# A hybrid encoder step on one core: split input-projection weights kept in DRAM and read back

## Chip, cores and metric

One core of a Trainium2 chip. The metric is the device time of one execution in microseconds (us).

## What is computed

One layer of a streaming encoder on 2,048 prompt tokens and 8 x 16 sample tokens (2,176 rows of width 1,024, fp32). The part that matters here is the first step: one input projection whose columns go to three token mixers.

```python
proj = jnp.einsum('btd,de->bte', x, lp['w_in'])
qa, ka, va, qkv_b, beta_in, a_in, gate_b, u_c = jnp.split(proj, split_points(IN_SIZES), axis=-1)
...
out_a = band_attention_prompt(qa, ka, va, lp['a_rel_bias'])
ob, s_new = gated_delta_rule(qb, kb, vb, g, beta, s0)
y_c, h_re, h_im = s5_ssm(u, ...)
mix = jnp.concatenate([out_a, out_b, out_c], axis=-1) @ lp['w_out']
x = layer_norm(DN_ALPHA * x + mix, ...)
hid = jnp.square(jax.nn.relu(x @ lp['w_up'] + lp['b_up']))
x = layer_norm(DN_ALPHA * x + hid @ lp['w_down'], ...)
```

## The kernel before

`w_in` is cut into eleven column blocks of 256 (one, called G, of 264). Every fp32 operand of a large matmul is used in two parts, both of type fp32r: the high part is a cast on ACT (L60), the low part is what is left of the number, by a subtract on DVE (L61). One product of two such operands is three matmuls (`mm3`, L65 to L67: high x high, low x high, high x low).

`weights` (L206) brings one block: two loads of 512 KB into `wr` (two buffers), and from these four pairs of tiles `wh`, `wl`, each 128 x 512, that is two of the block's eight slices of the inner dimension. `wh` and `wl` have five buffers each, so that one pair of the next block can be made while the four of this block are in use; each later pair waits until the matmuls no longer read the pair whose buffers it takes. `feat` (L230) multiplies a block with the transposed x (output: features by tokens, one PSUM tile per 128 features and group of tokens, 24 matmuls each); `tok` (L252) gives tokens by features (24 matmuls per 128 tokens). The outputs go by ACT to a tile `st` and by DMA to DRAM.

The blocks are used over and over. `project1` goes over three ranges of tokens (768, 768, 640) and uses six blocks in each: 0 (input of the S5 mixer), G, 1, 2, 3, 8. In the third range it goes on with the five blocks 6, 7, 9, 4, 5 (`project2`, for the last 640 tokens), and `project2_all` goes over the other three ranges of 512 tokens with the same five. That makes 38 uses of 11 blocks: 11 first uses and 27 later ones. Each use loads and splits its block anew.

Beside these matmuls run the chunked delta rule (`deltanet`: names `cin`, `s`, `blk`, `Ti`, `TU`, `bqs`, `brs`, `bps`), from the end of the first range on, and the S5 mixer (`s5`: `Tm`, `U`, `yq`, `s5p`) during `project2_all`. `mix` (L127) interleaves them; a scheduler then fixes the order of the instructions on each engine. Every engine works through its instructions in that order. All DMAs are issued by SP, on one queue; a DMA that waits holds up those behind it. The DMAs take eight completion semaphores in turn, so that each waits also for the landing of the DMA eight places before it.

After this first part come attention, the output projection and the feed-forward part; the change touches none of their lines.

Of the kernel before, what the change touches and what calls it, by code (L numbers as in the profile page):

```python
# [9 lines left out]
F32 = mybir.dt.float32  # L10
F32R = mybir.dt.float32r
# [30 lines left out]
class K:  # L42
# [88 lines left out]
    def mix(self, upto):  # L131
        nc, A = self.nc, self.A
        bes, ses = ExitStack(), ExitStack()
        self.bp = self.pool("bp", 3, PSUM, es=bes, side="right")
        self.brp = self.pool("brp", 1, PSUM, es=bes, side="right")
        self.pp = self.pool("pp", 2, PSUM, es=ses)
        self.s5p = self.pool("s5p", 2, PSUM, es=ses)
        self.flip = 0
        self.parts_done = 0
        deltanet = self.deltanet()  # L140
        self.s5c = self.pool("s5c", 1, es=ses)
        with ExitStack() as es:
            dense = self.project1(es)
            next(dense)
            self.s5_setup()
            for _ in range(5):
                next(dense)
            self.parts_done = 1
            self.b_consts(bes)
            self.b_pools(bes)  # L150
            due = 0.0
            for i, _ in enumerate(dense):
                if i in (5, 11):
                    self.parts_done += 1
                due += PACE1 if i < 12 else PACE1B
                while due >= 1:
                    next(deltanet)
                    due -= 1
        with ExitStack() as es:
            self.merge((self.project2_all(es), 1.0), (deltanet, PACE_B), (self.s5(), PACE_C))  # L160
        nc.sync.dma_start(A["o_k"], self.kT[3])
        nc.sync.dma_start(A["o_v"], self.vS[3])
        ses.close()
        bes.close()
# [38 lines left out]
        self.w_p = self.pool(f"wp{n}", 3, es=es)  # L203
        self.st_p = self.pool(f"st{n}", 2, es=es)

    def weights(self, src, n=256):  # L206
        out = []
        for a in range(2):
            wr = self.w_p.tile([128, 4, n], F32, name="wr", tag="wr", bufs=2)
            self.nc.sync.dma_start(wr, src[:, a * 4:a * 4 + 4])  # L210
            for b in range(0, 4, 2):
                wh = self.w_p.tile([128, 2, n], F32R, name="wh", tag="wh", bufs=5)
                wl = self.w_p.tile([128, 2, n], F32R, name="wl", tag="wl", bufs=5)
                self.split(wh, wl, wr[:, b:b + 2])
                out += [(wh[:, k], wl[:, k]) for k in range(2)]
        return out

    def load_x(self, t0, groups):
# [10 lines left out]

    def feat(self, idx, x, groups, out, by_group=False, w=None):  # L230

        w = w or self.weights(self.A["w_inA"][idx])
        todo = [(m, z) for m in range(2) for z in range(len(groups))]
        if by_group:
            todo.sort(key=lambda mz: mz[1])
        for m, z in todo:
            n = groups[z][1]
            ms = slice(m * 128, (m + 1) * 128)
            ps = self.pp.tile([128, 512], F32, name="pps", tag="pp")
            for k in range(8):  # L240
                self.mm3(ps[:, :n], w[k][0][:, ms], w[k][1][:, ms], *x[k, z], k == 0, k == 7)
            out(m, z, ps[:, :n])
# [23 lines left out]
    def project1(self, es):  # L266

        nc, A = self.nc, self.A
# [2 lines left out]
        up = [upp.tile([128, 16, NC5], F32, name=f"up{m}") for m in range(2)]  # L271
        self.p_pools(es, 1)
        for j, (t0, T, groups) in enumerate(PARTS):
            w = self.weights(A["w_inA"][0])
            x = self.load_x(t0, groups)

            def keep_u(m, z, ps):
                n0, n = groups[z]
                c0 = (t0 + n0) // 16
                v = ps.rearrange("p (c t) -> p t c", t=16)  # L280
                nc.scalar.copy(up[m][:, 0:8, c0:c0 + n // 16], v[:, 7::-1])
                nc.vector.tensor_copy(up[m][:, 8:16, c0:c0 + n // 16], v[:, 15:7:-1])

            def keep_v(t, st):
                v, rows = self.at_a(self.vS, t0 // 128 + t)
                nc.sync.dma_start(v[rows, 0:256], st[:, :256])
                nc.sync.dma_start(self.baS[j][t * 128:t * 128 + 128], st[:, 256:264])

            self.feat(0, x, groups, keep_u, by_group=True, w=w)
            yield 2  # L290
            self.tok(A["w_inG"], 264, x, groups, keep_v)
            yield 2
            for i in range(3):
                self.feat(1 + i, x, groups, self.to_rows(self.bT[j], i * 256, 0, groups))
                yield 2
            self.feat(8, x, groups, self.to_rows(self.gT[j], 0, 0, groups), by_group=True)
            yield 2
            if j == 2:
                yield from self.project2(3, x, groups)
# [4 lines left out]
    def project2(self, j, x, groups):  # L304

        n = sum(n for _, n in groups)
# [4 lines left out]
        for a in range(2):  # L311
            self.feat(6 + a, x, groups, self.to_rows(self.kT[j], a * 256, 0, groups))
            yield n / 384
        self.tok(self.A["w_inA"][9], 256, x, groups, keep_v)
        yield n / 384
        for a in range(2):
            self.feat(4 + a, x, groups, self.to_rows(self.qT[j], a * 256, 0, groups, -0.125))
# [1617 lines left out]
```

## Time and profile before

| | |
|---|---|
| median of 3 runs | 2851.4 us (2848.71 to 2852.71) |
| profiled execution, its own time | 2849.91 us |
| its span in the profile | 2848.1 us |
| granted TensorE clock, mean | 0.991 |
| busy share of the span: PE, PEld, DVE, ACT, POOL | 96%, 84%, 68%, 46%, 36% |
| chain of work that ended last | PE 68%, DVE 16%, DMA 6%, issue 4%, ACT 3%, POOL 2%, SP queue 1% |
| moved by DMA | 355.55 MB, mean 125 GB/s |

The span is divided by what the code does: the projections with the delta rule and S5 end at about 920 us of the span, and everything after that is untouched. So the change is to be read in the first 920 us. PE is the matmul row, PEld the loading of its stationary operands. A matmul of 384 columns is shown as some 340 ns long although the next one starts 175 ns later; the busy share of PE therefore says little, the start times say more.

### The profile page before, as it was taken

To read this page: it belongs to the slowest core of one execution; us is meant where nothing else is said; L and a number is where in the kernel's file an instruction comes from. 1 tells how busy PE (TensorE), PEld (TensorE's weight loads), DVE (VectorE), ACT (ScalarE), POOL (GpSimd) and SP (SyncE) were. 2 spreads that over 40 slices of the span, in tenths; PEclk is the share of its full clock that TensorE was granted. 3 is DMA by queue.
4 is the path that set the end of the run, shared out by engine and by line. 5 is a ranking of instruction groups with operands and counts; after the bars stand their busy time and mean duration, and the time that the engine had idled before them with its cause. 6 is when DMAs were issued, how large, how long until landed. Compare 5 with 4: busy or idle time off the path is not lost.

```text
span 2848.1 us, 46357 instructions
## 1 busy us (share of the span) xinstructions
PE 2738.6 (96%) x16685; PEld 2405.1 (84%) x16685; DVE 1945.4 (68%) x4949; ACT 1305.6 (46%) x2714; POOL 1032.7 (36%) x914
## 2 busy tenths in 40 slices
PE   8999999989989899999999999999999999999998
PEld 8988888867677677788898998989989988999997
DVE  7587888788653788879855555576556557576766
ACT  3554554343355778612243443355334435444443
POOL 0010111232221232013354445345544453666664
PEclk9999999989999999999999999999999999999999
DMA  5644445555447652145631221153222214432321
GB/s 185 204 111 120 111 114 125 150 147 155 146 138 247 213 167 61 55 169 198 224 124 60 74 75 59 60 196 131 88 74 86 93 67 148 163 98 95 119 96 46
DMA packets 293436, 355.55 MB, mean 125 GB/s; under 512 B 85698, under 2 KB 218646, under 8 KB 292886
## 3 DMA queue, kind: packets, MB, share of 16 engines
q1 hardware_dynamic: 293206, 352.59, 39.4%
q8 instruction: 131, 2.15, 0.3%
q14 instruction: 99, 0.81, 0.1%
HBM read 280.25 MB, written 74.89 MB: 125 GB/s over the span
## 4 chain that ended last, share of the span: by engine, by line
PE 68%; DVE 16%; DMA 6%; issue 4%; ACT 3%; POOL 2%; SPq 1%; DVEq 0%; ACTq 0%; POOLq 0%
PE fdp L66 8%; PE fdp L65 8%; PE fdp L67 8%; PE pps L66 2%; PE pps L67 2%; PE pps L65 2%; PE fupz L67 2%; PE fupv L67 2%; PE fupv L65 2%; PE fupv L66 2%; PE fupz L65 2%; PE fupz L66 2%; PE fupx L65 2%; PE fupx L67 2%; PE fupx L66 2%
## 5 line engine op out<-in xcount | busy, mean ns | idle before, releaser
L1570 POOL TENSOR_TENSOR wu<-wur,wu 128x512 fp32r<-128x512 f32 x308 | 416.7, 1357 | 528.1 <-ACT wu L1569 527.4
L1696 DVE TENSOR_TENSOR fy<-fy,fdp 128x512 f32<-128x512 f32 x500 | 340.9, 685 | 255.8 <-PE fdp L67 255.5
L65 PE MATMUL fdp<-wdh,hh 128*128 128x512 f32 x1020 | 397.8, 390 | 1.2 <-DVE fy L1696 1.1
L66 PE MATMUL fdp<-wdl,hh 128*128 128x512 f32 x1020 | 397.3, 390 | 0.1
L67 PE MATMUL fdp<-wdh,hl 128*128 128x512 f32 x1020 | 397.1, 389 | 0.0
L1569 ACT CAST wu<-wur 128x512 fp32r<-128x512 f32 x308 | 189.6, 617 | 414.1 <-DMA wur<-in_w_upL 168.6
L65 PE MATMUL pps<-xh,wh 128*128 128x384 f32 (+2 forms) x800 | 279.6, 351 | 10.5 <-ACT xh L60 9.5
L66 PE MATMUL pps<-xl,wh 128*128 128x384 f32 (+2 forms) x800 | 279.3, 349 | 2.4 <-DVE xl L61 2.3
L67 PE MATMUL pps<-xh,wl 128*128 128x384 f32 (+2 forms) x800 | 277.1, 347 | 0.7 <-DVE wl L61 0.7
L65 PEld LDWEIGHTS fdp<-wdh,hh 128*128 128x128 f32 x1020 | 191.4, 188 | 41.0 <-DVE fy L1696 2.9
L67 PEld LDWEIGHTS fdp<-wdh,hl 128*128 128x128 f32 x1020 | 191.5, 188 | 40.0
L66 PEld LDWEIGHTS fdp<-wdl,hh 128*128 128x128 f32 x1020 | 191.5, 188 | 38.5 <-DVE wdl L61 0.7
L1643 DVE TENSOR_TENSOR hl<-fre,hh 128x384 fp32r<-128x384 f32 (+1 forms) x180 | 143.4, 797 | 85.1 <-ACT hh L1642 84.4
L60 ACT CAST wdh<-wdr 128x1024 fp32r<-128x1024 f32 x94 | 98.8, 1051 | 205.6 <-PE fdp L67 205.2
L65 PEld LDWEIGHTS pps<-xh,wh 128*128 128x128 f32 x800 | 151.9, 190 | 23.3 <-ACT xh L60 11.3
L61 DVE TENSOR_TENSOR wl<-wr,wh 128x512 fp32r<-128x512 f32 (+1 forms) x152 | 107.5, 716 | 86.3 <-ACT wh L60 84.2
L66 PEld LDWEIGHTS pps<-xl,wh 128*128 128x128 f32 x800 | 151.8, 190 | 14.3 <-DVE xl L61 5.5
L67 PEld LDWEIGHTS pps<-xh,wl 128*128 128x128 f32 x800 | 151.5, 189 | 12.4 <-DVE wl L61 2.5
L61 DVE TENSOR_TENSOR wdl<-wdr,wdh 128x1024 fp32r<-128x1024 f32 x94 | 133.1, 1421 | 6.6 <-ACT wdh L60 6.6
L60 ACT CAST wh<-wr 128x512 fp32r<-128x512 f32 (+1 forms) x152 | 92.3, 618 | 79.9 <-DMA wr<-in_w_inA 41.4
L1638 ACT ACTIVATE fre<-fre,ld_b_up 128x384 f32<-128x384 f32 (+1 forms) x144 | 85.9, 597 | 63.3 <-DVE fre L1647 40.3
L1229 ACT ACTIVATE P<-P,st 128x640 f32<-128x640 f32 (+4 forms) x128 | 97.2, 760 | 30.2 <-DVE st L1226 29.6
(569 smaller groups left out, 7241.7 us busy)
## 6 DMA issues: line engine op xcount, KB each, us to landing
wdr<-in_w_dnL SPq DMA_DIRECT2D x96, 512.0 KB
wur<-in_w_upL SPq DMA_DIRECT2D x88, 512.0 KB
wr<-in_w_inA SPq DMA_DIRECT2D x70, 512.0 KB
TU<-tD SPq DMA_DIRECT2D x34, 256.0 KB
y<-in_x SPq DMA_DIRECT2D x17, 512.0 KB
x<-y SPq DMA_DIRECT2D x17, 512.0 KB
fxr<-x SPq DMA_DIRECT2D x17, 512.0 KB
fy<-x SPq DMA_DIRECT2D x17, 512.0 KB
```

Source lines behind the costliest of these rows:

```text
L60: nc.scalar.copy(hi, src)
L61: nc.vector.tensor_tensor(lo, src, hi.bitcast(F32), OP.subtract)
L65: mm(out, lh, rh, start=first, stop=False, **kw)
L66: mm(out, lh, rl, start=False, stop=False, **kw)
L67: mm(out, ll, rh, start=False, stop=last, **kw)
L1229: self.nc.scalar.activation(x, x, AF.Exp, scale=-1.0, bias=st[:, q:q + 1], accum_out=st[:, 2 + q:3 + q])
L1569: self.nc.scalar.copy(hi, src)
L1570: P.tensor_tensor(lo, src, hi.bitcast(F32), OP.subtract)
L1638: nc.scalar.activation(r, src, AF.Relu, bias=self.bu[:, c * 2 + i:c * 2 + i + 1])
L1643: V.tensor_tensor(hl, r, hh.bitcast(F32), OP.subtract)
L1696: V.tensor_tensor(y, y, ps[x], OP.add)
```

## The change

`weights` now takes the number of the block (None for G) and keeps, per block, four DRAM tiles of 2 x 128 x 512. At the first use of a block it loads and splits as before and then writes the high and the low part of each pair to DRAM: eight DMAs of 256 KB. At every later use it neither loads nor splits; it reads the eight parts back straight into `wh` and `wl`.

```diff
+        self.wD = {}
...
-    def weights(self, src, n=256):
+    def weights(self, i, n=256):
+        nc = self.nc
+        first = i not in self.wD
+        if first:
+            self.wD[i] = [self.dram.tile([2, 128, 2 * n], F32, name=f"wD{i}_{a}") for a in range(4)]
         out = []
-        for a in range(2):
-            wr = self.w_p.tile([128, 4, n], F32, name="wr", tag="wr", bufs=2)
-            self.nc.sync.dma_start(wr, src[:, a * 4:a * 4 + 4])
-            for b in range(0, 4, 2):
-                wh = self.w_p.tile([128, 2, n], F32R, name="wh", tag="wh", bufs=5)
-                wl = self.w_p.tile([128, 2, n], F32R, name="wl", tag="wl", bufs=5)
-                self.split(wh, wl, wr[:, b:b + 2])
-                out += [(wh[:, k], wl[:, k]) for k in range(2)]
+        for a in range(4):
+            w = wh, wl = [self.w_p.tile([128, 2, n], F32R, name="w" + q, tag="w" + q, bufs=5) for q in "hl"]
+            if first:
+                if a % 2 == 0:
+                    wr = self.w_p.tile([128, 4, n], F32, name="wr", tag="wr", bufs=2)
+                    src = self.A["w_inG"] if i is None else self.A["w_inA"][i]
+                    nc.sync.dma_start(wr, src[:, a * 2:a * 2 + 4])
+                b = a % 2 * 2
+                self.split(wh, wl, wr[:, b:b + 2])
+            for q in range(2):
+                t = w[q].rearrange("p k n -> p (k n)").bitcast(F32)
+                if first:
+                    nc.sync.dma_start(self.wD[i][a][q], t)
+                else:
+                    nc.sync.dma_start(t, self.wD[i][a][q])
+            out += [(wh[:, k], wl[:, k]) for k in range(2)]
         return out
```

The calls pass the number in place of the source. Of the DMAs of `weights`, 76 loads of `wr` before become 22 loads, 88 writes and 216 reads of 256 KB.

How the instructions move shows at two places of SP's queue. The first is the start of the program (`xr` is a raw tile of x, of which the first product needs eight). Before:

```order
L71 DMA ld_c_ident<-in_c_ident 128x128
L210 DMA wr<-in_w_inA 128x1024 x2
L225 DMA xr<-in_xT 128x384 x6
L71 DMA ld_s_are<-in_s_are 128x16
L71 DMA ld_s_aim<-in_s_aim 128x16
```

After:

```order
L71 DMA ld_c_ident<-in_c_ident 128x128
L221 DMA wr<-in_w_inA 128x1024 x2
L240 DMA xr<-in_xT 128x384 x4
L227 DMA wD_0_126<-wh 128x512
L227 DMA wD_0_126<-wl 128x512
L227 DMA wD_1_127<-wh 128x512
L227 DMA wD_1_127<-wl 128x512
L227 DMA wD_2_128<-wh 128x512
L227 DMA wD_2_128<-wl 128x512
L227 DMA wD_3_129<-wh 128x512
L227 DMA wD_3_129<-wl 128x512
L240 DMA xr<-in_xT 128x384 x12
```

Eight writes, each of which waits for its half of a split, now stand between the fourth and the fifth tile of x.

The second place is the change from block G to block 1 in the second range (`st_2154` and `st_2218` are G's fifth tile of tokens; `blk`, `cin`, `DT` belong to the delta rule; in brackets the semaphores waited for). Before:

```order
L210 DMA wr_2900<-in_w_inA 128x1024 [waits DMAHW0_49,DVE_49]
L505 DMA cin_2744<-bT0_60 128x131 [waits DMAHW1_49,DMAHW2_49,DVE_49,Activation_49]
L605 DMA aD_81<-at_1965 64x4x64 [waits DVE_49]
L605 DMA aD_81<-at_1965 64x4x64 [waits DMAHW3_49]
L286 DMA vS2_76<-st_2183 128x256 [waits DMAHW4_49,Activation_49]
```

After:

```order
L229 DMA wh_2519<-wD1_1_832 128x512 [waits DMAHW7_49,PE_49]
L621 DMA blk_1738<-aD_81 32x16x16 [waits DMAHW4_49,DMAHW3_49,DMAHW0_49]
L301 DMA vS2_76<-st_2247 128x256 [waits DMAHW1_49,Activation_49]
L302 DMA baS1_79<-st_2247 128x8 [waits DMAHW2_49]
L229 DMA wl_2520<-wD1_1_832 128x512
L229 DMA wh_2523<-wD1_2_833 128x512 [waits PE_49]
L229 DMA wl_2524<-wD1_2_833 128x512 [waits DMAHW5_49]
L229 DMA wh_2527<-wD1_3_834 128x512 [waits DMAHW6_49,PE_49]
L229 DMA wl_2528<-wD1_3_834 128x512 [waits DMAHW7_49]
L520 DMA cin_2804<-bT0_60 128x131 [waits DMAHW0_49,DVE_49]
```

Where a load into `wr` waited for DVE to be done with the raw tile, reads into `wh` and `wl` now wait for PE to be done with the pair before, with the delta rule's loads behind them.

## Rows read from the trace of the kernel before

**Rows 1.** Stretches, us from the start: busy time and instructions by engine, clock, DMA
```profile
core 0: us, PE busy (x) PEld busy (x) DVE busy (x) ACT busy (x) POOL busy (x), PEclk, DMA share, GB/s
0.00:30.00 30.00, 21.12 (x114) 20.44 (x115) 22.32 (x100) 16.62 (x35) 0.20 (x4) 1.00 0.79 254
30.00:98.00 68.00, 67.84 (x425) 67.12 (x424) 38.79 (x150) 18.94 (x37) 1.55 (x6) 1.00 0.60 175
98.00:430.00 332.00, 319.58 (x2385) 286.65 (x2384) 268.15 (x1069) 177.50 (x457) 46.15 (x53) 1.00 0.45 124
430.00:580.00 150.00, 145.50 (x1090) 126.87 (x1089) 115.57 (x442) 59.45 (x153) 32.72 (x69) 1.00 0.49 133
580.00:860.00 280.00, 247.59 (x1513) 199.06 (x1512) 204.97 (x607) 119.31 (x260) 72.23 (x95) 0.95 0.52 151
860.00:920.00 60.00, 58.91 (x301) 48.65 (x299) 17.53 (x30) 30.17 (x56) 6.39 (x6) 1.00 0.79 256
```

**Rows 2.** Costliest groups of the page: the splits of the weights
```profile
L61 DVE TENSOR_TENSOR wl<-wr,wh 128x512 fp32r<-128x512 f32 (+1 forms) x152 | 107.5, 716 | 86.3 <-ACT wh L60 84.2
L60 ACT CAST wh<-wr 128x512 fp32r<-128x512 f32 (+1 forms) x152 | 92.3, 618 | 79.9 <-DMA wr<-in_w_inA 41.4
```

**Rows 3.** Waits, 0 to 920 us: total us, times, longest us
```profile
ACT wh L60 <- PE pps L66: 28.6, 36, 4.1
...
SPq L210 <- DVE wl L61: 26.2, 20, 6.2
```

**Rows 4.** Waits of PE, 98 to 430 us
```profile
PE brs L786 <- DVE Ti L627: 2.7, 3, 1.5
...
PE pps L67 <- DVE wl L61: 0.3, 1, 0.3
```

**Rows 5.** Chain of waits by line: of 98 to 430 us, then of 580 to 920 us
```profile
by line: issue 11.3%; PE bqs L649 8.7%; PE pps L67 7.1%; PE pps L66 7.1%; PE pps L65 6.9%; DVE s L512 5.7%; DVE tp L625 2.9%; DMA wr<-in_w_inA 2.7%; PE brs L692 2.7%; PE brs L690 2.6%; DVE Ti L627 2.6%; DVE wl L61 2.5%; PE brs L694 2.3%; PE
...
by line: issue 7.0%; DMA yq<-yS 5.5%; PE pps L66 5.1%; PE pps L67 4.9%; PE pps L65 4.8%; DMA rv<-in_relrev 4.2%; DMA Tm<-kS 3.8%; DMA xr<-in_xT 2.8%; PE s5p L1019 2.4%; DVE s L512 2.3%; DVE wl L61 2.3%; PE bqs L649 2.2%; DVE xl L61 2.2%; SP
```

**Rows 6.** Pieces of that chain: start us, us, what
```profile
226.66 4.45 DMA wr<-in_w_inA
...
231.13 0.63 ACT wh L60
...
231.79 0.69 DVE wl L61
...
238.63 3.60 DMA TU<-tD
...
288.61 5.26 DMA xr<-in_xT
```

**Rows 7.** Timeline of the start: SP's issues and ACT's first casts
```profile
2.12 3.09 SPq L225 DMA_DIRECT2D xr<-in_xT  x6
...
7.79 2.85 ACT L60 CAST xh<-xr 128x384 fp32r<-128x384 f32 x6
```

**Rows 8.** Timeline of PE: matmuls of 384, of 264 and of 512 columns
```profile
12.20 0.34 PE L66 MATMUL pps<-xl,wh 128*128 128x384 f32 x1
...
14.14 0.34 PE L65 MATMUL pps<-xh,wh 128*128 128x384 f32 x1
14.31 0.34 PE L66 MATMUL pps<-xl,wh 128*128 128x384 f32 x1
...
27.92 0.28 PE L65 MATMUL pps<-wh,xh 128*128 128x264 f32 x1
28.04 0.29 PE L66 MATMUL pps<-wl,xh 128*128 128x264 f32 x1
...
902.22 0.39 PE L66 MATMUL pps<-xl,wh 128*128 128x512 f32 x1
902.45 0.39 PE L67 MATMUL pps<-xh,wl 128*128 128x512 f32 x1
```

**Rows 9.** DMA issues: KB each
```profile
TU<-tD SPq DMA_DIRECT2D x34, 256.0 KB
```

More of the change, by code (lines that the diff above doesn't have):

```diff
@@ L230, in feat @@
     def feat(self, idx, x, groups, out, by_group=False, w=None):
-        w = w or self.weights(self.A["w_inA"][idx])
+        w = w or self.weights(idx)
         todo = [(m, z) for m in range(2) for z in range(len(groups))]
@@ L273, in project1 @@
         for j, (t0, T, groups) in enumerate(PARTS):
-            w = self.weights(A["w_inA"][0])
+            w = self.weights(0)
             x = self.load_x(t0, groups)
@@ L290, in project1 @@
             yield 2
-            self.tok(A["w_inG"], 264, x, groups, keep_v)
+            self.tok(None, 264, x, groups, keep_v)
             yield 2
@@ L313, in project2 @@
             yield n / 384
-        self.tok(self.A["w_inA"][9], 256, x, groups, keep_v)
+        self.tok(9, 256, x, groups, keep_v)
         yield n / 384
```

## The prediction

> **What bounds the kernel now.** I read first the stretches of the span, cut where the code goes from one kind of use to the other [rows 1]: 0 to 98 us holds the first uses of six blocks, 98 to 430 us twelve later uses, 430 to 580 us five first uses, 580 to 920 us fifteen later ones. The reader is to see that PE is the engine in use nearly all the time. In 98 to 430 us it is idle for 332.0 - 319.6 = 12.4 us and its weight loads for 45.4 us; in 580 to 860 us for 32.4 and 80.9 us; before 98 us (the first 30 us apart) and from 860 us on it is hardly idle at all. DVE is second, at 268.2 of 332.0 us. DMA has room in the middle (shares 0.45 to 0.52) and little at both ends (0.79).
>
> Then the groups of instructions [rows 2]: each split is a cast of 618 ns on ACT and a subtract of 716 ns on DVE. Then who waits for whom. The casts wait 36 times for PE to free a pair, 28.6 us in all, and SP's loads 20 times for DVE to be done with a raw tile, 26.2 us [rows 3]; but PE waits directly for a low part for only 0.3 us in 98 to 430 us, and its longest item there is 2.7 us [rows 4]. The splits matter through the chain instead: in those two stretches it runs through `wl` for 2.5% of 332 and 2.3% of 340 us [rows 5], because DVE takes its work in order and the delta rule's small operations stand behind `wl`. One such place is shown [rows 6]: a load of 4.45 us, a cast of 0.63, a subtract of 0.69, and the solve goes on only then.
>
> **What the change removes (G).** 27 later uses x 4 splits = 108 casts and 108 subtracts: 108 x 0.618 = 66.7 us of ACT and 108 x 0.716 = 77.3 us of DVE [rows 2]. On the chain this is at most 2.5% x 332 + 2.3% x 340 = 16.1 us of `wl`, some 4 us of `wh` (7 pieces of 0.6 us, of which one is shown [rows 6]) and 2.7% x 332 = 9.0 us of `wr` [rows 5]: 29 us. The gain lies between 0, where PE is busy anyway, and 29 us. Since PE is idle for only 12.4 us in the first of the two stretches and waits there for other things [rows 1, 4], I take 8 us: nearer to the direct waits than to the chain.
>
> **The start (S).** The eight writes of block 0 now stand ahead of the fifth tile of x. Before, six tiles were issued from 2.12 us on, and their casts ran without a gap from 7.79 us [rows 7], so that the fifth was cast at about 7.8 + 4 x 0.475 = 9.7 us. The writes are 8 x 0.262 = 2.1 MB; 254 GB/s at a share of 0.79 [rows 1] is 322 GB/s at full share, so they take 6.5 us, and the fifth tile comes at about 16.2 us. The first four tiles give PE 24 matmuls, which end at about 12.2 + 12 x 0.175 = 14.3 us (twelve had been started by 12.20 us, 0.17 us apart from there on [rows 8]). The rest is a stall of 2 us, 3 with the tile's own split. Bounds: 0, if the writes start late enough to let x pass in the DMA engines, and 8, if all eight tiles of the second group come late too. PE is full until 98 us, so this is not made up. I take 3 us.
>
> **Later first uses (F).** Blocks G, 1, 2, 3, 8 write 10.5 MB in 30 to 98 us, 154 GB/s on top of 175 GB/s. That stretch moved 175 GB/s at a share of 0.60, so full share is between 292 GB/s and the 322 of the start [rows 1]: 329 GB/s needs 1.02 to 1.13 times the stretch, 1 to 8 us more. Loads made ahead for the second range can give way; lower bound 0, I take 3. The writes of 430 to 580 us (10.5 MB, 70 on top of 133 GB/s at 0.49) find room: 0, covered by PE, which is full there; without that cover they would be late by their own 7 parts in 100 of the stretch at most. A write waits for its split, and behind it on SP stand stores and the next block's load, which is still a whole use (17 us of PE) ahead.
>
> **The read-backs (B), the largest term.** A pair may be overwritten only when the last output tile of the use before has gone past it. Matmuls of 384 columns start 0.175 us apart, of 264 0.12, of 512 0.23 [rows 8]; a pair serves six of them, so in the last tile of 24 the pairs come free 1.05, 0.73 or 1.37 us apart. The first pair of the next block has spare buffers; the second, third and fourth don't. Before, ACT and DVE refilled such a pair in 0.62 + 0.72 = 1.3 us. Now a DMA does. The trace has no such read; the nearest row is `TU`, of the same 256 KB [rows 9], which landed after 3.60 us [rows 6]. The second half follows 0.262 MB / 322 GB/s = 0.8 us later, and so does each further one.
>
> For 384 columns the second pair is full at 1.05 + 3.6 + 0.8 = 5.45 us from the start of the last tile, the fourth at 8.65; PE wants them at 4.2 + 1.05 = 5.25 and 4.2 + 3.15 = 7.35. That is 1.3 us late. After G (last tile 2.9 us) it is 2.3 us; from one block to the next at 512 columns the fourth is full at 8.97 and wanted at 5.5 + 4.1 = 9.6, so in time; after a block of `tok` 1.3 us late. The uses: 10 x 1.3 + 2 x 2.3 + 3 x 1.3 + 12 x 0 = 21.5 us, if nothing stands between. But about half of the 2,385 matmuls in 98 to 430 us are the delta rule's [rows 1], and they stand between the projection's: I take two thirds, 14 us. Lower bound 0. Upper bound: a load that shared the queue landed after 5.26 us instead of 3.6 [rows 6]; 1.66 us more at each change gives 10 x 3.0 + 2 x 4.0 + 3 x 3.0 + 12 x 1.1 = 60 us.
>
> The Trainium skill, "DMA: Bandwidth & Descriptors", section "Anatomy of one DMA", gives a fit of about 2.0 us plus the bytes at 436 GB/s (measured on another issuing path), 2.6 us for 256 KB; the row says 3.60, and the sum goes by the row. By the page each change would be 1.0 us earlier and B an estimated 4 us.
>
> The added wait and what is behind it: the read waits at SP's head for PE, and behind it stand the other half, the delta rule's `blk` and `cin` and stores of `st`. Loads waited there before too, for DVE [rows 3]. 250 more DMAs also wait each for the landing of the eighth before. I put nothing on this beyond the bounds of B.
>
> **The end of the part (T).** From 860 us on PE is full and the projections run alone; 5.5 uses read 1.05 MB more each, 96 on top of 256 GB/s, which is 352 against 256 / 0.79 = 324 GB/s [rows 1]: 60 x 352 / 324 = 65 us, 5 more. Loads for attention can give way: 0 to 6, I take 3. The Trainium skill, same page, section "Where 436 GB/s comes from", puts the ceiling of the DMA engines at 435 GB/s; by it there would be room, and T would be 0. The row bears out only 324, by its busy share.
>
> **Sum.** S 3 + F 3 + B 14 + T 3 - G 8 = 15 us. On the profiled execution's 2849.9 us this is 2864.9; the median of the runs is 1.5 us above that execution, so I predict **2866 us**. A difference under 0.2% (5.7 us) is about what a measurement of this kernel can't tell from no change.
>
> **Rivals.**
> - *The vector engines are freed and the reads hidden (faster).* The chain's 29 us come off, since no `wl` stands ahead of the solve any longer, and the delta rule's matmuls cover B but for 3 us: 2851.4 - 29 + 3 + 6 (S and T) = 2831 us. For it: DVE at 268 of 332 us, and the piece at 226 us [rows 1, 6]. Against it: the 12.4 us that PE has to give there, and PE's own waits [rows 4]. It decides if pairs land before PE comes to them, that is within 3.1 us of being freed at 384 columns.
> - *Gain and cost cancel (same).* B 3 and G 8 with S and F and T as above in part: 2851.4 - 8 + 3 + 6 = 2852 us. For it: matmuls of another kind at every change of block.
> - *The queue becomes the bound (much slower).* Reads that wait for PE hold SP, each landing comes late by the upper bound: S 8, F 8, B 60, T 3, no gain but 8: 2851.4 + 71 = 2922 us. For it: the 5.26 us row; against it: shares of 0.45 and 0.52 in the stretches with later uses [rows 1].
>
> That the change doesn't do what it says is excluded by the order of the instructions (22 loads, 88 writes, 216 reads).
>
> **How the numbers follow.** Chances: forecast 0.46, freed engines 0.25, cancel 0.17, queue 0.12. Faster 0.25, same 0.17, slower 0.46 + 0.12 = 0.58. The forecast's own range is 2856 to 2890. The range given, 2834 to 2904, takes in the forecast and "cancel" and part of the other two: of "faster" its smaller gains, of "queue" its lower end; some 0.2 stay outside.
>
> **What would show it.** ACT's casts and DVE's subtracts of weights fall from 152 to 44 each, DVE in 98 to 430 us by about 35 us. PE's first wait after the start is for a cast of x, near 14 to 17 us. In the stretches with later uses PE's waits on projections name a DMA out of the kept tiles, 0.5 us each on average. The part ends near 935 us; the rest of the span takes as long as before. The prediction is wrong if PE's idle time in 98 to 430 us falls below 12 us (then G is larger and B hidden), or if SP's waits for PE come to more than 100 us (then the queue bounds).

## The result, and the profile after

| | before | after |
|---|---|---|
| median of the runs | 2850.7 us (2848.7 to 2852.7) | 2922.8 us (2921.4 to 2923.9) |
| span of the profiled execution | 2848.1 us | 2922.0 us |
| granted TensorE clock, mean | 0.991 | 0.979 |

The change makes the kernel 1.0258 times as long (95% interval 1.0245 to 1.0271), 72 us. The forecast was 15 us: the sign was right, the size far off, and the time lies outside the range.

The page of the kernel after: engines, DMA queue, chain by engine. Then the splits of the weights, by tile (count, shortest/median/longest ns, first and last start).

```profile
PE 2766.0 (95%) x16685; PEld 2423.2 (83%) x16685; DVE 1891.3 (65%) x4841; ACT 1250.4 (43%) x2606; POOL 1030.7 (35%) x914
...
q1 hardware_dynamic: 329206, 404.12, 43.7%
...
PE 69%; DVE 13%; DMA 8%; ACT 3%; issue 3%; POOL 2%; SPq 1%; DVEq 0%; ACTq 0%; POOLq 0%
```

```profile
L61 DVE TENSOR_TENSOR wl<-wr,wh x44: 673/690/701, 6.3 to 621.0; 128x512 fp32r<-128x512 f32 x40, 128x528 fp32r<-128x528 f32 x4
```

The 108 subtracts are gone, and DMA's share of the chain has gone from 6% to 8%. Where the time went is read by stage. The start of the last evacuation of a use (ACT's copy of its last PSUM tile, a row of the timeline) is the same event in both traces. It comes at 117.3 us before and 121.3 after for the last first use of range one, 460.7 and 511.8 for the end of the third range's first six blocks, 597.0 and 640.7 for that of its five further ones, 626.5 and 695.6 for the first use of `project2_all`, 856.4 and 914.4 for the tenth, 919.9 and 983.7 for the last. So the shift is **4, 51, 44, 69, 58, 64 us**, and the first result of attention is 74 us later. From there on both kernels take 1917 us. All of the loss stands in the first part, and it comes in steps. In the middle the shifts are not lost time alone, since other work changes places too: by 511.8 us PE has done 1,404 matmuls that aren't the projections', by 460.7 us before 1,310. By the tenth use of `project2_all` it has done 2,581 in both.

The stretches of [rows 1], in the kernel after, cut at the same events, and one more up to attention (PE, PEld, DVE, ACT, POOL busy; clock; DMA share; GB/s):

```profile
0.00:32.00 32.00, 20.88 (x98) 19.42 (x98) 18.78 (x79) 15.83 (x34) 0.20 (x4) 1.00 0.83 272
32.00:104.00 72.00, 69.58 (x429) 68.94 (x430) 42.37 (x167) 18.12 (x35) 1.55 (x6) 0.98 0.83 274
104.00:466.00 362.00, 333.18 (x2391) 297.64 (x2389) 247.88 (x1041) 154.87 (x412) 44.93 (x53) 0.95 0.55 156
466.00:626.00 160.00, 151.71 (x1137) 131.66 (x1137) 119.63 (x454) 61.45 (x158) 34.78 (x71) 0.98 0.60 174
626.00:918.00 292.00, 248.33 (x1467) 199.29 (x1467) 174.09 (x537) 94.45 (x212) 65.70 (x93) 0.92 0.64 194
918.00:984.00 66.00, 59.97 (x297) 47.97 (x295) 7.04 (x14) 16.78 (x31) 1.04 (x2) 1.00 0.81 271
984.00:1005.00 21.00, 13.49 (x62) 7.98 (x62) 6.28 (x36) 11.98 (x34) 7.90 (x10) 0.58 0.73 220
```

Two things are to be seen. PE's idle time in the stretch of the twelve later uses is 362.0 - 333.2 = 28.8 us; it was 12.4 [rows 1]. And the clock column falls below 1.00 in five of the seven rows; before it did so in one of six. A share of 0.95 over 362 us is 36 us at half the clock (only 0.5 and 1 occur); the rows add up to about 110 us, those of before to about 36 up to the same event. PE was busy in 78 us of these (27 before).

The 74 us up to attention's first result have two parts. PE is idle for 107.9 us, and was for 62.9: 45 us. And it is busy for 896.8 us, and was for 867.5, with the same matmuls: 29 us. At half the clock a matmul of 384 columns starts 0.32 us after the last one in place of 0.175 (rows below), so the 51 us more of work at 1.2 GHz in place of 2.4 cost an estimated 23 us of these 29.

PE's waits, 0 to 1005 us (total, times, longest), and SP's:

```profile
PE bqs L664 <- DMA TU<-tD: 15.8, 3, 10.9
PE pps L65 <- ACT xh L60: 10.6, 3, 8.5
PE pps L65 <- DMA wh<-wD: 8.3, 7, 3.9
PE s5p L984 <- DVE WB L979: 7.1, 1, 7.1
...
PE pps L66 <- DMA wl<-wDNone: 5.2, 2, 3.4
...
PE pps L67 <- DMA wl<-wD: 2.5, 6, 0.9
```

```profile
SPq L229 <- PE pps L67: 19.7, 29, 4.1
...
SPq L227 <- ACT wh L60: 16.0, 10, 3.3
```

With two small groups (1.3 and 0.7 us) the waits that name a read-back come to 18.0 us. SP's waits for PE at the reads are 19.7 us, and 7 more on another semaphore, far under the 100 us that the prediction had named as the sign of a bound by the queue.

How a late refill looks, on PE's timeline (in brackets the idle time before the row and what ended it):

```profile
186.47 0.45 PE L67 MATMUL pps<-xh,wl 128*128 128x384 f32 x1 [0.93 <-DMA wl<-wD]
...
187.10 0.50 PE L67 MATMUL pps<-xh,wl 128*128 128x384 f32 x2
188.55 0.69 PE L65 MATMUL pps<-xh,wh 128*128 128x384 f32 x1 [0.95 <-DMA wh<-wD]
189.03 0.52 PE L66 MATMUL pps<-xl,wh 128*128 128x384 f32 x1
189.35 0.52 PE L65 MATMUL pps<-xh,wh 128*128 128x384 f32 x1
...
191.90 0.34 PE L66 MATMUL pps<-xl,wh 128*128 128x384 f32 x1
192.07 0.34 PE L65 MATMUL pps<-xh,wh 128*128 128x384 f32 x1
```

After the wait the matmuls start 0.32 us apart, where [rows 8] have 0.175 for this size, and from 191.90 on 0.17 again: the granted clock is 0.5 from 188.5 to 191.9 us. A wait of 0.95 us cost some 1.5 us more in slow matmuls.

The refills themselves, pieces of the chain of waits from 117 to 480 us (start, us, what):

```profile
122.82 4.26 DMA wl<-wD
...
143.50 5.87 DMA wh<-wDNone
...
183.87 4.63 DMA wh<-wD
...
253.35 2.90 DMA wl<-wD
```

Seven such pieces stand in that stretch, 2.9 to 5.9 us long, 4.1 in the mean; the forecast took 3.6 us from `TU` [rows 6]. The Trainium skill, "DMA: Bandwidth & Descriptors", section "Anatomy of one DMA", has a fit, measured on another issuing path, by which 256 KB take an estimated 2.6 us; the measured pieces decide against it here.

The first step behind the first range, 10 us at the first use of the second (24.1 us long, 14.1 before): PE waits for the first pair of block 0, and SP issues its read only at the end of the first range, where the load of block 0 had gone out 21 us ahead. PE and SP after, then SP before:

```profile
125.08 0.66 PE L65 MATMUL pps<-xh,wh 128*128 128x384 f32 x1 [3.85 <-DMA wh<-wD]
```

```profile
121.11 0.82 SPq L229 DMA_DIRECT2D wh<-wD  x1
```

```profile
96.47 0.38 SPq L210 DMA_DIRECT2D wr<-in_w_inA  x1
```

What stands ahead of it in the queue, constants and the zeroing of `tD`, went out from 71 to 94 us before and goes out from 83 to 121 us now; up to 105 us SP waits some 20 us for halves to be written. The granted clock is 0.5 from 123.6 to 130.4 us.

The largest single step, 25 us at the first use of `project2_all`: SP's issues, then PE.

```profile
638.34 3.06 SPq L264 DMA_DIRECT2D qT<-st  x2
641.44 1.81 SPq L317 DMA_DIRECT2D uS<-up  x3
656.18 1.90 SPq L650 DMA_DIRECT2D tD<-Ti  x4
658.19 2.07 SPq L651 DMA_DIRECT2D TU<-tD  x4
660.32 0.97 SPq L240 DMA_DIRECT2D xr<-in_xT  x2
661.33 0.43 SPq L229 DMA_DIRECT2D wh<-wD  x1
```

```profile
640.28 0.28 PE L67 MATMUL pps<-xh,wl 128*128 128x256 f32 x1
647.62 1.11 PE L984 MATMUL s5p<-ld_c_ident,WB 128*128 128x128 f32 x4 [7.06 <-DVE WB L979]
648.66 1.89 PE L990 MATMUL s5p<-ZC,st 128*16 128x256 f32 x4
661.42 1.97 PE L664 MATMUL bqs<-at,TU 128*128 128x64 f32 x8 [10.87 <-DMA TU<-tD]
```

The projections end at 640.6 us. SP then stands from 643.3 to 656.2 before the delta rule's `tD`, which waits for DVE to finish `Ti`, and the tiles of x for the next range stand behind it. PE has nothing else to do: two holes of 7.1 and 10.9 us, and the clock at 0.5 until 673 us. Before, x was issued from 593.8 us, ahead of `tD` and `TU`. No read-back is late here; the scheduler's order on SP is another. Of the 25 us some come back: 71 more matmuls of other work stand ahead of the end of this use than before, and by the tenth use the shift is 58.

### The profile page after: what moved, and what is told of

It is laid out like the page before. It is cut to its first block, busy times and chain, and to the rows that moved or that the text cites. A ratio compares the mean times of both kernels' runs of the same rounds, so it can differ in the third digit from the quotient of the medians.

```text
span 2922.0 us, 46500 instructions
## 1 busy us (share of the span) xinstructions
PE 2766.0 (95%) x16685; PEld 2423.2 (83%) x16685; DVE 1891.3 (65%) x4841; ACT 1250.4 (43%) x2606; POOL 1030.7 (35%) x914
## 3 DMA queue, kind: packets, MB, share of 16 engines
q1 hardware_dynamic: 329206, 404.12, 43.7%
## 4 chain that ended last, share of the span: by engine, by line
PE 69%; DVE 13%; DMA 8%; ACT 3%; issue 3%; POOL 2%; SPq 1%; DVEq 0%; ACTq 0%; POOLq 0%
PE fdp L66 8%; PE fdp L65 8%; PE fdp L67 8%; PE pps L67 3%; PE pps L66 3%; PE pps L65 3%; PE bqs L664 2%; PE fupv L67 2%; PE fupv L65 2%; PE fupv L66 2%; PE fupz L65 2%; PE fupz L67 2%; PE fupz L66 2%; PE fupx L65 2%; PE fupx L67 2%
## 5 line engine op out<-in xcount | busy, mean ns | idle before, releaser
L67 PEld LDWEIGHTS pps<-xh,wl 128*128 128x128 f32 x800 | 153.0, 191 | 16.7 <-DMA wl<-wD 6.2
L66 PEld LDWEIGHTS pps<-xl,wh 128*128 128x128 f32 x800 | 153.2, 192 | 12.4 <-DVE xl L61 3.1
L199 ACT ACTIVATE st<-pps 128x384 f32<-128x384 f32 (+3 forms) x122 | 57.1, 468 | 206.0 <-PE pps L67 164.1
L1241 DVE CUSTOM_DVE_ANT_0 P<-aps,nb 128x128 f32<-128x128 f32 (+3 forms) x128 | 60.3, 483 | 78.8 <-PE aps L1240 78.5
```

What stands on the lines that cost most here:

```text
L66: mm(out, lh, rl, start=False, stop=False, **kw)
L67: mm(out, ll, rh, start=False, stop=last, **kw)
L1241: self.nc.vector.tensor_tensor_reduce(x[:, x0:x0 + n], ps[:, d0:d0 + n], nb[:, x0:x0 + n], 1.0, low, OP.add, OP.min, st[:, q:q + 1])
```

## Experiments

The theories, as the expectations name them. **R**: refills are late, because a pair can be read back only after PE has freed it. **Q** and **B**: places in the queue, and bytes. **O**: the scheduler's other order, at `project2_all` above all, where x stands behind `tD` and `TU`. **H**: a write that waits for its split holds the queue, and the loads behind it can no longer run ahead. Shifts are against before, at the events named above; "over before" is the median less that of before, measured beside it on the same chip. The edits are given in short.

### Which half of the change costs

**Writes alone.** Every later use loads and splits as before.

```diff
-            if first:
+            if True:                     # load wr and split, always
...
-                else:
-                    nc.sync.dma_start(t, self.wD[i][a][q])
```

> First uses write their 88 halves to DRAM, but the later uses load and split as before; nothing is read back. Theory R (refills come late: a pair can be read back only after PE has freed it, lands 3 to 5 us later, PE stalls and then runs at half its clock): only the start and the first uses pay, as in the profile after, where the evacuations were 4 to 8 us later up to 121 us; total 4 to 10 us over before, 2855 to 2861 us, PE's half-clock time in the first 930 us near that of before (46 us). Theory Q (250 more DMAs and 86 MB more on one queue hold up all the others): 88 of the 250 cost their share of the 72 us, some 25 us: 2876 us. Theory O (the scheduler puts other work behind other work; above all x of project2_all stands behind the delta rule's TU on SP): in this program x stands ahead of TU again, so the step of 25 us at the first use of project2_all is gone.

Measured: 2890.1 us, ratio 1.014 (1.0124 to 1.0156), 40 us over before. R's price for the writes, 4 to 10 us, holds only up to 121 us (shift 4.4). Then the first use of the second range takes 26.0 us against 14.1, the shift is 29.7 us at the end of the third range and 42 at the tenth use of `project2_all`. So 40 us come without any read-back. O's sign is there too: no step at the first use of `project2_all` (the shift falls from 29.7 to 27.1 us).

**Read-backs in project1's ranges only, and in project2_all only** (only the blocks used there are kept; for the second the condition is turned round).

```diff
-        first = i not in self.wD
+        first = i not in self.wD or i in (6, 7, 9, 4, 5)   # these: load, split, no write
```

> Only the six blocks of project1's ranges (0, G, 1, 2, 3, 8) are written and read back (48 writes, 96 reads, 12 later uses); blocks 6, 7, 9, 4, 5 are loaded and split anew each time. Theory R: the shift at the last evacuation of block 8 in the third range is as in the profile after, 40 to 50 us, and then stays; total 2885 to 2900 us. Theory Q: 144 - 24 = 120 more DMAs of 250: about 35 us, spread evenly, 2885 us. Theory O: no step at project2_all, since x stands ahead of TU here; the total is 20 to 30 us under that of the change.

> Only the five blocks of project2 (6, 7, 9, 4, 5) are written and read back (40 writes, 120 reads, 15 later uses); the first ranges are as before. Theory R: uses of 512 columns cover their refills but for the end; total within 8 us of before, 2843 to 2859 us. Theory Q: 160 - 30 = 130 more DMAs of 250: about 37 us, 2888 us. Theory O: no step at project2_all, x stands ahead of TU.

Measured: 2896.8 us (1.0145 to 1.0186), 46 us over before, and 2882.2 us (1.0087 to 1.0126), 32 us. The first has the shifts of the change up to the end of the third range (52.0, 42.6; the change 51.1, 43.7) and then only 4 us at the first use of `project2_all`, and nothing at the end: 47.5 us at the tenth use, 46 in all; that is R's time, and O's difference to the change (26 us) as well. The second is 4.4 us off when the third range ends (11 at one use before), then loses 15 us at the first use of `project2_all` and, from the tenth use to the end, goes from 13.9 to 31.6. R's 8 us for it was wrong. The expectation was wrong about the order, too: four of the eight tiles of x stand behind `tD` and `TU` in this program.

**Seven buffers in project2_all** (the raw tiles aren't needed there).

```diff
         self.w_p = self.pool(f"wp{n}", 3, es=es)
+        self.w_bufs = 5 if n == 1 else 7         # and bufs=self.w_bufs for wh and wl
```

> As rb_p2, with seven buffers for each half in project2_all in place of five (the raw tiles are not needed there). Theory R: refills start one or two pairs earlier, the waits of PE on read-backs go to nearly nothing and the last five uses lose less: 3 to 8 us under rb_p2, 2840 to 2852 us. Theory Q: the same DMAs on the same queue, so the same time as rb_p2 within 3 us.

Measured: 2874.4 us (1.0066 to 1.0099), 8 us under the one with five, the upper end of R's 3 to 8; the same DMAs on the same queue. R's difference holds, Q's doesn't; R's total is missed, since the 15 us at the first use stay.

### The writes: queue, bytes or order

**Writes issued by ACT**, without and with the read-backs (these on SP, then on ACT too), and the kernel of the last paragraph on ACT's queue: the write's `nc.sync` becomes `nc.scalar`, or the read's as well.

```diff
-                    nc.sync.dma_start(self.wD[i][a][q], t)
+                    nc.scalar.dma_start(self.wD[i][a][q], t)
```

> As w_only (first uses write, nothing is read back), but ACT issues the 88 writes in place of SP. Theory H (head of the line: on SP a write waits for its split, the split for PE to free the pair, and the loads behind it, x of the second range first of all, can't run ahead any more): SP runs ahead as in the kernel before, x of the second range is issued from about 105 us and not from 123, PE's wait for a cast of x there falls from 8.5 to under 2 us; total 2851 to 2860 us against 2890 of w_only. Theory B (bytes: 23 MB more writes take the DMA engines): the bytes are the same, so 2880 us or more. Theory O (the scheduler's other order alone): the order changes again, no direction is forecast, so anything from 2845 to 2890.

> The change with the 88 writes issued by ACT; the 216 reads stay on SP. Theory H with R (refills come late): the part of w_only goes (some 40 of 72 us), the part of the reads stays, 20 to 35 us: 2871 to 2886 us. Theory R alone: 2910 us or more.

> The change with writes and reads all issued by ACT. If what the reads cost comes of SP being held by them (theory H for the reads too), it is 10 us or more under w_act_r_sp, 2850 to 2870 us. If it comes of their landing late after PE frees the pair (theory R), it is as w_act_r_sp within 6 us, and PE's waits that name a read-back come to 12 us or more. If waits of ACT for PE hold up the evacuations behind them, it is slower than w_act_r_sp.

> Only the five blocks of project2 kept, writes and reads issued by ACT, seven buffers for each half in project2_all. Theory H with R: no late x, refills a pair or two ahead, 60 casts and 60 subtracts less: 2838 to 2856 us, against 2874 of the same with all on SP (rb_p2_b7). Theory B: 2868 us or more.

Measured: 2884.1 us (1.0098 to 1.014), 2909.3 (1.0193 to 1.0232), 2928.3 (1.0255 to 1.0301) and 2879.0 (1.0082 to 1.013): 33, 58, 77 and 28 us over before. All four miss H's times. By time alone the first and the last lie where B had put them, and the second just under R alone's 2910; the third is slower than the second, as waits of ACT would have it. But H's own sign is there: in the first kernel x goes out 10.8 us before the first range ends (11.8 before, 1.8 us after it with the writes on SP), PE waits for nothing there, and the first use of the second range takes 16.7 us, not 26.0. (The wait of 8.5 us that the expectation names is PE's at the start of the program, 8.3 us before; with the writes on SP, PE waits at this place 6.8 us for a cast of block 0, whose load goes out at 121.2 us.) The holding moved to ACT's queue. ACT at the start of the first of these kernels (`ACTq`: its DMA issues):

```profile
8.83 0.33 ACTq L229 DMA_DIRECT2D wD<-wh  x1
9.89 0.33 ACTq L229 DMA_DIRECT2D wD<-wl  x1
...
15.60 0.33 ACTq L229 DMA_DIRECT2D wD<-wl  x1
15.97 2.58 ACT L60 CAST xh<-xr 128x384 fp32r<-128x384 f32 x6 [4.57 <-DMA wD<-wl]
```

The casts of x, at 7.79 us before [rows 7], stand behind eight writes that wait for their halves and for semaphores, until 15.97 us; the first use of all is 11 us late, where writes on SP made it 1.7. With the reads on ACT as well, PE's waits for `xh` and `TU` grow from 18.3 and 3.6 us to 26.5 and 13.6.

**Writes of 4 KB** on SP, 88 of them with the same waits; **the kernel before with 54 copies of 512 KB** beside its loads; **the same with 4 KB**.

```diff
-                    nc.sync.dma_start(self.wD[i][a][q], t)
+                    nc.sync.dma_start(self.wD[i][a][q][:, 0:8], t[:, 0:8])
```

```diff
                     nc.sync.dma_start(wr, src[:, a * 2:a * 2 + 4])
+                    if not first:                # DRAM to DRAM
+                        nc.sync.dma_start(dd, src[:, a * 2:a * 2 + 4])
```

> As w_only, with the 88 writes on SP cut to 8 of 512 columns each (4 KB in place of 256 KB): the same DMAs with the same waits in the queue, 23 MB less. What is written is read by nobody. Theory H (a write that waits for its split holds SP, and the loads behind it come late): the start and the second range lose as in w_only, 15 us or more by the last evacuation of the second range's block 0 (147.7 us there, 131.3 before); total 2870 to 2890 us. Theory B (bytes at the start and in the first uses): 2850 to 2858 us. In between, 7 us at the start are bytes and some 10 at the second range's x are the queue.

> The kernel before with each of the 54 loads of a later use doubled by a 512 KB copy from DRAM to DRAM on SP, which nothing waits for and which waits for nothing but its semaphore: the bytes of the read-backs, without a wait for PE. Theory R (refills late after PE frees the pair): nothing of the read-backs' cost shows, within 8 us of before, 2843 to 2860 us, apart from the tail, where DMA was at a share of 0.79. Theory B: 27 MB more in the same stretches cost what the read-backs cost, 25 us or more: 2876 us.

> The kernel before with 54 DMAs of 4 KB more on SP, one beside each load of a later use; they wait for nothing but their semaphore, and the order of PE is the same as before. Theory H (what costs in the queue is waiting for a split or a pair, not a place in it): within 5 us of before, 2843 to 2856 us. If places in the queue and the eight semaphores are the cost, 54 of 250 are worth 7 us or more: 2858 us or more.

Measured: 2882.7 us (1.0096 to 1.0126), 2868.1 (1.0037 to 1.0071) and 2855.2 (1.0007 to 1.0026): 32, 17 and 5 us over before. So 88 writes of 4 KB cost 32 of the 40 us, as H's total has it, and 54 DMAs that wait for nothing cost 5. The copies of 512 KB miss both forecasts: 17 us is more than R's 8 and less than B's 25. They don't price bytes alone, since the size of a DMA changes the scheduler's order: compared place by place, by the names of their tiles, 3,399 of PE's 16,685 matmuls stand elsewhere than before with the copies of 512 KB, and 4 with those of 4 KB. In its place the loss of the small writes isn't H's either: by the first use of the second range the shift is 6.5 us, where H expected 15 and the full writes have 16.4. There the bytes count: x of the second range is issued from 105.4 us before, from 113.2 with small writes, from 123.5 with full ones, from 126.3 in the change. The 10 to 12 us at this place need both: with small writes on SP this use takes 16.3 us, with full ones on ACT 16.7, with full ones on SP 26.0. SP's first issue of x for the second range, before and after:

```profile
105.44 3.73 SPq L225 DMA_DIRECT2D xr<-in_xT  x6
```

```profile
126.33 8.52 SPq L240 DMA_DIRECT2D xr<-in_xT  x10
```

The remaining shift of the small writes builds up in the second and third range (25 us at 486 us), where they no longer write; their program has another order there.

**Another order by itself:** one constant of the interleaving of `mix` changed in the kernel before, one in each run.

```diff
-PACE_C = 1.2
+PACE_C = 1.15
...
-PACE1B = 1.25
+PACE1B = 1.15
```

> The kernel before with one constant of the interleaving changed, PACE_C 1.15 in place of 1.2 (S5 a little earlier against the projections in project2_all); the work is the same. It measures what another order alone is worth. Theory O (any other order in project2_all costs 15 to 25 us there, because the one before was fitted): 2862 us or more, with the loss between the first and the second use of project2_all. Theories H, R and B: same as before, 2846 to 2856 us.

> The kernel before with one constant of the interleaving changed, PACE1B 1.15 in place of 1.25 (the delta rule runs a little slower beside the five blocks at the third range's end); the same work, no DMA more. It measures what the delta rule's place at the change to project2_all is worth by itself. Theory O: the loss between the last use of the third range and the second use of project2_all that all runs with writes have (12 to 22 us) appears here too: 2862 us or more. If it is the writes themselves: 2846 to 2856 us.

Measured: 2853.1 us (0.9999 to 1.0018) and 2853.2 (1.0015 to 1.0033): 2 and 7 us over before. A mild reordering costs little; O as a general rule (any other order loses 15 us or more) falls. But these two are mild: 118 and 815 of PE's matmuls stand elsewhere, against 3,936 in the change and 3,194 with the writes alone. A reordering of that size without the DMAs was not run, so what it costs by itself is not shown.

### The step at project2_all, and the late refills

**Fewer kept blocks near the change to project2_all.** First 6, 7 and 9 alone kept (six buffers in `project2_all`), then all but 4 and 5:

```diff
-        first = i not in self.wD
+        first = i not in self.wD or i in (4, 5)     # and no write for these
```

> Only blocks 6, 7 and 9 kept, the first three of project2 (24 writes, 72 reads, 9 later uses), on SP, six buffers for each half in project2_all; blocks 4 and 5, whose writes stood last before project2_all, are loaded and split anew. Theory H: x of project2_all is no longer behind writes, so the 15 us that rb_p2 lost between the last use of the third range and the first of project2_all go: 2848 to 2860 us. Theory O: another order, the loss there stays at 10 us or more: 2865 us or more.

> The change without keeping blocks 4 and 5, the last two before project2_all (72 writes and 168 reads left; their 8 uses load and split as before). In this program all but two of the tiles of x for project2_all stand ahead of the delta rule's tD and TU on SP; in the change they stand behind. Theory O: the step of 25 us at the first use of project2_all shrinks to under 10, and the total falls by 15 to 25 us to 2898 to 2908 us. Theory R alone (refills): two of project2_all's five blocks no longer read back, worth some 3 us: 2918 us or more.

Measured: 2873.0 us (1.0054 to 1.0087) and 2899.1 (1.0168 to 1.0202): 22 and 53 us over before. In the second the shift is 41.0 us when the third range ends (43.7 in the change) and 43.1 after the first use of `project2_all` (69.1): the 25 us are gone, with 168 of 216 reads still there. Its SP at that place:

```profile
636.51 0.41 SPq L242 DMA_DIRECT2D xr<-in_xT  x1
638.33 0.32 SPq L266 DMA_DIRECT2D qT<-st  x1
638.70 0.42 SPq L242 DMA_DIRECT2D xr<-in_xT  x1
...
652.80 2.02 SPq L652 DMA_DIRECT2D tD<-Ti  x4
```

x goes out from 636.5 us, ahead of `tD`, and PE's longest wait there is 3.8 us. The edit also drops 16 writes and 48 reads, but the step goes with the order and not with these, as all the kernels together show. How many of the eight tiles of x that the first use needs stand ahead of `tD` on SP, and how much the shift grows in that use:

| tiles ahead of `tD` | kernels | growth of the shift, us |
|---|---|---|
| 8 | twelve, writes alone and project1's read-backs among them | -2.6 to 3.9 |
| 6 | blocks 4 and 5 not kept, with five and with six buffers | 2.2, 1.5 |
| 4 | project2's blocks alone on SP, with five and with seven buffers | 14.7, 14.6 |
| 1 | one DMA per pair | 25.8 |
| 0 | the change; more buffers everywhere | 25.4, 28.9 |

So this step is the order on SP: shown. In time it is worth some 19 us, by which the second kernel is less over before than the change. In the first of the two kernels the step also goes (shift 7.8 and then 6.7 us), but 17 us come at the second use, so its total misses H; it is O's total, without O's place.

**More buffers everywhere:** six in project1 (x's raw tiles cut from six to four), seven in `project2_all`. **One DMA per pair:** both halves in one tile, 512 KB. **Six buffers and blocks 4 and 5 not kept.** The edits of the first two:

```diff
-        self.xr_p = self.pool(f"xr{n}", 6 if n == 1 else 2, es=es)
+        self.xr_p = self.pool(f"xr{n}", 4 if n == 1 else 2, es=es)
...
+        self.w_bufs = 6 if n == 1 else 7
```

```diff
-            for q in range(2):
...
-                    nc.sync.dma_start(t, self.wD[i][a][q])
...
+            w = self.w_p.tile([128, 2, 2, n], F32R, name="w", tag="w", bufs=5)
...
+                nc.sync.dma_start(t, self.wD[i][a])
```

> The change with six buffers for each half in project1's ranges (x's raw tiles cut from six to four to make room) and seven in project2_all. Theory R: refills start a pair or two earlier; PE's 18 us of waits that name a read-back fall to under 9, less half-clock time follows from it, and the last five uses lose 6 us less; total 2895 to 2910 us. The order at project2_all is the bad one of the change (x behind TU), so its step of 25 us stays. Theory O alone: nothing in particular, within 8 us of the change, 2915 to 2930 us.

> The change with both halves of a pair in one tile and one DMA of 512 KB for it: 44 writes and 108 reads in place of 88 and 216; the bytes are the same. If the number of DMAs on SP's queue, each waiting for the landing of the eighth before, is what costs, half of the change's loss goes: 2880 to 2895 us. Theory R: a refill of 512 KB lands about when the second half of a pair did, so the waits of PE on read-backs stay at 15 us or more and the total is within 12 us of the change, but for the order at project2_all, where here two DMAs of x stand ahead of tD and the rest behind.

> Both cures at once: blocks 4 and 5 not kept (skip45, 24 us under the change) and six buffers for each half everywhere, x's raw tiles cut to four (rb_all_b67, 17 us under it). If the step at project2_all and the late refills are two separate costs, they add: 2876 to 2888 us, and what is left over before, 30 to 40 us, is what the writes cost (w_only lost 40). If the order made both, they don't add: 2893 us or more.

Measured: 2905.7 us (1.0183 to 1.0214), 2910.1 (1.0202 to 1.0232) and 2885.0 (1.0109 to 1.0139): 59, 64 and 35 us over before. With more buffers PE's waits that name a read-back, and the stretch of the twelve later uses:

```profile
PE pps L67 <- DMA wl<-wD: 2.9, 2, 2.2
...
PE pps L65 <- DMA wh<-wD: 1.6, 3, 0.7
```

```profile
104.00:449.00 345.00, 325.16 (x2399) 291.44 (x2398) 252.57 (x1042) 155.65 (x413) 43.64 (x53) 1.00 0.58 164
```

The waits fall from 18.0 to 4.5 us, the idle time from 28.8 to 19.8, the clock comes back from 0.95 to 1.00, and the stretch is 17 us shorter. The bad step at `project2_all` is still there (26.0 to 54.8 us), as expected. R is shown for this stretch, and the slow clock there goes with the late refills. At the end R misses: the last five uses lose 5.0 us, hardly less than the change's 5.8. Half the DMAs save 8 us, far from Q's half of the loss, and the waits come to 13.8 us, a little under R's 15. Both cures together: alone they take 19 and 13 us off the 72 against before, which would leave 40; measured 35. They add up as two separate costs would. What is left is near what the writes alone cost (40), though this kernel has 72 of the 88.

## Why the prediction was wrong

The direction was right; the sum of 15 us was not, against 72. Its counted waits came out about as forecast. What failed is the step from a load that gives way, or a short wait, to nothing further: the loads of the next range, x at `project2_all` and attention's loads came late, and the granted clock fell after waits.

- **S and F, 6 us:** 4.1 us by the last first use of the first range. The fifth tile of x was cast at 14.60 us (16.2 forecast). Right as far as they went. The step that failed is the sentence "Loads made ahead for the second range can give way", priced at nothing: they gave way (block 0's weights by 25 us, x by 21), and the second range's first use took 24.1 us in place of 14.1. 10 us. A side sum of F is wrong as well: 10.5 MB at 292 to 322 GB/s are 22 to 24 parts in 100 of the stretch of 430 to 580 us, not 7; it made no difference, the shift doesn't grow there.
- **B, 14 us:** PE's direct waits are 18.0 us, 0.67 per use (0.5 forecast). The term as counted was right; what it left out is that PE then runs at half its clock. More buffers gave back 17 us of the stretch of the twelve later uses (13 us of the whole), and all but 4.5 us of the waits. So what B stood for cost some 13 to 17 us, inside its bounds of 0 to 60; the clock was in none of the terms.
- **G, -8 us:** the subtracts of weights in the stretch of the twelve later uses fell by 33 us (35 forecast), DVE's work by 20, since more of the delta rule's falls into it. No stage shows a gain that the runs tell from a change of order. Its lower bound, 0, was nearer.
- **T, 3 us:** from the tenth use of `project2_all` to the end the change loses 14 us (58.0 to 72), 6 in the projections, the rest up to attention's first results. Kernels without reads there lose nothing (writes alone 42.0 to 39.6, project1's read-backs 47.5 to 46.3). The term was mis-sized: the loads for attention were not free to give way. The first load of its queries goes out 2.4 us before the projections end, before it was 14.8 us, and PE waits 6.6 us for their casts and low parts, where it had not waited. The reads of the last uses are late besides (3.9 us of PE's waits, forecast in time at 512 columns). SP before, then after:

```profile
905.09 0.44 SPq L1174 DMA_DIRECT2D qr<-qT  x1
```

```profile
981.35 0.42 SPq L1189 DMA_DIRECT2D qr<-qT  x1
```

- **Not in the sum:** 25 us where x fell behind `tD` and `TU` at `project2_all`. The prediction looked at the order at two places, and not at this one, though the same comparison shows it there. Some 19 us in the end.
- **The rivals:** "the queue becomes the bound" gave 2922 us, the measured time, by luck, from other terms: its 60 us of B and its SP that waits for PE aren't there (27 of the 100 us named). The one piece of it that is true is that the queue is in order, and that what waits in it holds what could run ahead. "Freed engines" fell: PE waits more, not less. "Cancel" fell with the direction.
- **The signs named:** splits 44 (right), PE's first wait for a cast of x (at 17.5 us, 0.4 us long), the part's end near 935 us (983.7), the rest as long as before (74 us late at attention's first result, then equal).

Left open, some 20 to 30 of the 72 us: what makes most of the 32 us of the small writes, in the second and third range, and the 6 to 15 us that most of the kernels with x ahead lose over the first three uses of `project2_all`. Each has its own order there, and of the kernels with DMAs added only the one with 54 small ones held PE's order. The writes and the other order are both possible causes. No version beat the kernel before.

## What to carry to other kernels

Before replacing on-chip work by a read, look at what the old way had ready when a buffer came free: here raw tiles were in SBUF and a refill took 1.3 us from PE's release, while a read could only start then and took 2.9 to 5.9. Where one queue in order carries all DMAs, a store that waits for its producer also delays the loads behind it that used to run ahead (10 to 12 us at one change of range here, when the stores were large as well), and at each change of stage one has to read whose load now stands behind whose wait. Count a stall of PE at more than its length if the granted clock falls after it.

## What was not expected of the hardware

Short waits can cost clock. In the first 1005 us the granted clock fell to 0.5 twelve times, for 3.4 to 27.3 us, against six times up to the same event before; when it fell at 188.5 us PE had stood for refills twice, 0.93 us up to 186.47 and 0.95 us up to 188.55. The Trainium skill, "TensorE: Matmul & The Clock Gate", section "HAM oscillation — how this bites in real kernels", tells of a kernel whose waits for DMA put each next group of matmuls at the lower clock, and reckons half of the throttled time as the loss; by that the additional 51 us of matmuls at 0.5 cost an estimated 26 us, and this trace agrees: PE's busy time for the same matmuls grew by 29 us.

Moving DMAs to another engine's queue moved the waiting with them: ACT's casts stood behind its own writes until 15.97 us. With the writes on ACT the change was 58 us over before in place of 72, and x stood ahead of `tD` there; with the reads on ACT too it was the slowest kernel of all, 77 us over before.
